# A hybrid decoder layer on one core: copies moved from VectorE to ScalarE, two heads scaled in one product, priorities at stage borders, new step orders

## The chip, the cores and the metric

The kernel runs on one core of one Trainium2 chip. The core has a matrix engine (TensorE, "PE" in the profile, with its weight loads as "PEld"), a vector engine (VectorE, "DVE"), an activation engine (ScalarE, "ACT"), a general engine (GpSimd, "POOL") and an engine that here only issues DMAs (SyncE, "SP"). Each works through its own queue in order; semaphores make one wait for another. PSUM is the memory that matmuls write, in banks; SBUF holds everything else on the chip. The metric is the device time of one launch in microseconds.

## The reference

One layer of a decoder for a prompt of 2048 positions and for 8 sample sequences of 8 new positions, with shared weights, all in float32:

```python
h = rmsnorm(x, g_pre_mix)
proj = h @ w_in                                  # 1024 -> q 512 | k 128 | v 128 | u 512
q, k = rope(q, pos), rope(k, pos)
attn = sink_attention(...)                       # 8 query heads, 2 kv heads of 64, window 128, sinks
pooled = pool_mix(u_ext, pos, pool_w, pool_scale)   # trailing means over 2/4/8/16 minus the token
mix = concatenate([rmsnorm(attn, g_attn), rmsnorm(pooled, g_pool)]) @ w_out
x = x + rmsnorm(mix, g_post_mix)
hf = rmsnorm(x, g_pre_mlp)
ff = square(relu(hf @ w_up)) @ w_down            # 1024 -> 4096 -> 1024
x = x + rmsnorm(ff, g_post_mlp)
x = x + sigmoid(x @ w_ple_gate + b_ple_gate) * (pe @ w_ple)
```

In the softmax every row's sum also holds exp(sink - max). The outputs are both x, and the last 128 keys and values and the last 15 pooling inputs of the prompt and of each sample; the old part of the sample's state is copied over unchanged.

## The kernel before

Float32 products are split: an operand is written as a high part in the engine's short float32 form and a low remainder, and a product is three matmuls, high x high, high x low, low x high (`mm3`, L134 to L136). The splits are a cast on ScalarE (L207) and a subtraction on VectorE (L130).

The work runs in stages, one behind the other.

1. *Mixer* (to about 420 us). 16 prompt tiles of 128 positions, t = 0 to 15, behind the sample tile t = -1. For a tile, `front` does the input projection, keys and values first, then queries, then u, in some 14 steps; `attention` does the scores, the softmax and the products with the values in 6 steps, for the two groups g of four heads; `pooling` has 3 steps, `finish` (called `l` when it belongs to the tile before) 2. In the loop's turn t the front of tile t + 1 is woven with attention and pooling of tile t and the finish of tile t - 1. Which step comes next is written out by hand in strings: ORDER for most tiles, ORDERW for tiles 3 to 10, where the output weights are split and stored as well (`e`), ORDER1 for tile 14, ORDER2 for tile 15, where `e` is the first part of the output product.

   In `front` the transposed keys of a tile go into the right half of `kp`, and the keys of the tile before are copied into its left half (L462, VectorE). In `attention` the exponents `pr` of four heads are scaled by the reciprocal sums `es`, two by VectorE, two by ScalarE (L535, L537). The product with the values, `po`, holds for each group the sums of the high and of the low parts in two halves of 64 partitions; one half is copied to `part` (L560, VectorE), and VectorE adds the other half to it (L561). Banks of PSUM rotate: two for transposes (`tr`), two for scores, two shared by `po`, pooling and the sums of squares (`o`), two for projections.

2. *Output product and first residual* (to about 607 us). `Mixed.product` makes two partial sums per half of the columns; ScalarE scales the first (L252), VectorE the second and adds it (L254). `first_residual` normalizes, adds x and writes the result. The residuals of the last two tiles are late: `residual_late(0)` and `residual_late(1)` are called inside the first round of the next stage, behind its steps p6 and p5.

3. *Up projection* (to about 1262 us). A scheme with seven products in place of eight for a 2 x 2 block matrix. 48 rounds, for three blocks of 352 columns and 16 column pairs of the weights. `up_weights` loads four blocks of a round's weights into `raw`, forms four differences (`diff`, L1016, in block 0) and splits the seven operands. A round runs its products p1, p2, p6, p7, p5 and, behind the next round's p1, the last two (`end`). `ahead`, called at a round's start, prepares the next round's weights. `snap` (L1059) is ScalarE's copy of a partial sum that the same bank goes on adding to, so the next product on that bank waits for it.

4. *Down projection* (to about 1902 us), in the same seven products (`DownQuad`), for 8 groups g of the weights' rows and 8 pairs tp of tiles, a quad each. VectorE adds each result to `z` (L1278). The next group's weights come in from tp = 2 on: two loads (L1211) at tp = 2, two at tp = 4, differences on GpSimd (L1217), splits. The sample rows are done at tp = 2 (`sample_down`, their sums at L1323 and L1325). In group 1 at tp = 3 three DMAs copy the sample's old state to the outputs.

5. *Second residual, gate and embedding* to the end.

Every instruction's place in its engine's queue is decided when the program is built, by a planner that simulates the run: of the instructions that are ready in its simulated time it takes the one that is earliest in the program. Under `tc.high_priority()` an instruction goes before the others that are ready; `tc.keep_in_program_order` pins an instruction behind what its engine was given before. DMAs are issued by SP in its queue's order.

Of the kernel before, what the change touches and what calls it, by code (L numbers as in the profile page):

```python
# [10 lines left out]
F32 = mybir.dt.float32  # L11
# [3 lines left out]
ALU = mybir.AluOpType  # L15
PSUM = bass.MemoryType.PSUM

P = 128
# [24 lines left out]

ORDER = "f f f f l f a f f p a f f f f f a f p f a f f l a a p"

ORDERW = "e a e f f l f f f f p a f f f e f a f f p a f f f f p a a l"
ORDER1 = "f a f f f l a f f f p f a f f f f f p l f a a a p"
ORDER2 = "e a p l a a e l a p e a e p e e"
# [40 lines left out]
def trunk(ctx: ExitStack, tc: tile.TileContext, i: dict, o: dict):  # L89
# [121 lines left out]
    class Mixed:  # L211
# [26 lines left out]
        def product(self, t, nh, bank, into=None):  # L238

            n = tn(t)  # L240
            m, z = self.m[t], self.z[t]
            ns = slice(nh * 512, nh * 512 + 512)
            pab = [bank.tile([P, 512], F32, tag="acc", name="pab") for _ in range(2)]
            for cg in range(2):
                for c in range(4):
                    wk = self.w[cg * 2 + c // 2, nh]
                    a = (m[:, 0, cg * 4 + c], m[:, 1, cg * 4 + c]) if t >= 0 else m[:, 0, cg * 4 + c]
                    mmt(t, pab[cg], a, (wk[:, c % 2, 0], wk[:, c % 2, 1]), c == 0, c == 3)
                if t < 0:
                    fold(into, pab[cg], "s", 2, 2048)  # L250
                if cg == 0:
                    A.mul(out=z[:n, ns], in_=pab[0][:n], mul=rap[:n, t + 1, 0:1])  # L252
                else:
                    V.scalar_tensor_tensor(  # L254
                        out=z[:n, ns], in0=pab[1][:n], scalar=rap[:n, t + 1, 1:2], in1=z[:n, ns], op0=ALU.mult, op1=ALU.add
                    )
                yield
# [16 lines left out]
    with ExitStack() as sa:  # L274
# [111 lines left out]
        def front(t, hT, cs, rs, res):  # L386
            n = tn(t)
# [62 lines left out]
            for j, _ in enumerate(gemm(768, 512, ups)):  # L450
# [3 lines left out]
                if j == 0:  # L454
                    kp = over.pool.tile([P, 4, 256], F32R, tag="kp", bufs=2, name="kp")
                    ps = tr.tile([P, 4, P], F32R, tag="tr", name="trk")
                    for g in range(2):
                        for e in range(2):
                            T.transpose(ps[:, g * 2 + e, :], khl[:, g, 2 * e : 2 * e + 2, :].rearrange("p a d -> p (a d)"), identr)
                    A.copy(out=kp[:, :, P:], in_=ps.bitcast(F32))  # L460
                    if t > 0:
                        V.tensor_copy(kp[:, :, :P], state["kp"][:, :, P:].bitcast(F32))  # L462
                    state["kp"] = kp
                    yield
# [26 lines left out]
        def attention(t, kp, qT, mix, sq):  # L491
# [5 lines left out]
            for g in range(2):  # L497
# [34 lines left out]
                V.reciprocal(es, es)  # L532
                for hh in range(4):
                    if hh % 2:
                        A.mul(out=pr[:, hh, :nkey], in_=pr[:, hh, :nkey], mul=es[:, hh : hh + 1])  # L535
                    else:
                        V.tensor_scalar_mul(pr[:, hh, :nkey], pr[:, hh, :nkey], es[:, hh : hh + 1])  # L537
                prs.append(pr)
                yield
            part = over.pool.tile([P, 4, P], F32, tag="part", bufs=1, name="part")  # L540
            for g in range(2):
# [17 lines left out]
                own, other = slice(g * HD, g * HD + HD), slice(HD - g * HD, 2 * HD - g * HD)  # L559
                V.tensor_copy(part[own], po[other])  # L560
                V.tensor_tensor(out=mix[own, 0:4, :], in0=po[own], in1=part[own], op=ALU.add)  # L561
# [255 lines left out]
    with ExitStack() as sb:  # L817
# [145 lines left out]
        with ExitStack() as s3:  # L963
# [37 lines left out]
            def up_weights(b, j):  # L1001
# [19 lines left out]
                rows(b22, 1, 1)  # L1021
                rows(b21, 1, 0)
                if b == 0:
                    diff(t1, t3, b11)
# [81 lines left out]
            def up_rounds():  # L1106
# [3 lines left out]
                o7s = {}  # L1110

                def prepare(k):
                    if k < len(rounds):
                        held[k] = list(zip(*zip(*(up_weights(b, j) for b, j in rounds[k]))))

# [3 lines left out]
                sp3.n = 1  # L1119
                o7s[0].update(load_ops(0, OPS[5:]))  # L1120

                behind = {
                    0: {"p6": lambda: residual_late(0), "p5": lambda: residual_late(1)},
                    1: {"p6": turn_late, "p5": turn_late},
# [3 lines left out]
                for k, r in enumerate(rounds):  # L1128
                    quads = [UpQuad(b, j, o7s[b], w) for (b, j), w in zip(r, held.pop(k))]
# [72 lines left out]
        with ExitStack() as s4:  # L1202
# [145 lines left out]
            def down_quads():  # L1348
# [4 lines left out]
                def quad(k):  # L1353
# [159 lines left out]
```

## Time and profile before

| | us |
|---|---|
| median of three runs (2151.54 to 2157.3) | 2156.13 |
| the profiled execution | 2156.64 |
| its span in the profile | 2154.9 |

The profile is of one execution. Its first part gives each engine's busy time. A row of the windows view gives, for a stretch from A to B, its length, then busy time (and count of instructions) for PE, PEld, DVE, ACT and POOL, then the granted clock of TensorE as a share of full speed, the DMA engines' busy share and GB/s. A row of the groups view gives line, engine, operation, output <- inputs, shapes and count, then busy time and the mean of one in ns, then the engine's idle time just before them and what ended it. A row of the waits view gives who waited for whom, us in total, how often, and the longest. A row of the timeline gives start, duration and instruction, and in brackets the engine's idle time before it and what ended it. Matmuls overlap: one's duration is longer than the distance from its start to the next one's. A few matmul records are missing from the trace.

### The profile page before, as it was taken

How to read it: one execution, taken by the hardware profiler on the slowest of the kernel's cores; microseconds unless marked ns; L12 is line 12 of the kernel's file. 1: busy time of each engine (PE TensorE's matmuls, PEld its weight loads, DVE VectorE, ACT ScalarE, POOL GpSimd, SP SyncE). 2: the span in 40 equal slices, each digit the busy share in tenths (PEclk: the TensorE clock that was granted, in tenths of full speed). 3: DMA queues.
4: the chain of work that ended last, by engine and by line, in shares of the span. 5: the costliest groups of instructions: out<-in, count | busy, mean ns of one | idle time of the engine just before them, and what ended most of it. 6: DMA issues, size and time to landing. Idle time of an engine off the chain costs nothing. (4 is left out here: it accounts for less than half of the span.)

```text
span 2154.9 us, 31214 instructions
## 1 busy us (share of the span) xinstructions
PE 2129.8 (99%) x11439; PEld 1882.8 (87%) x11439; DVE 1573.8 (73%) x2719; ACT 956.8 (44%) x1864; POOL 576.3 (27%) x643
## 2 busy tenths in 40 slices
PE   8999999999999999999999999999999999999999
PEld 6888888788889999999999988788888888888887
DVE  6899888876688777555755566788888888876553
ACT  5676666545455445444544455233232233232221
POOL 2334343343440000000000035534534544300000
PEclk9999999999999999999999999999999999999999
DMA  7552122768789668666766532231231222342211
GB/s 221 176 174 92 63 70 67 264 220 249 230 259 322 223 217 273 208 191 190 225 197 189 164 111 92 97 101 49 92 99 53 97 91 72 107 138 83 89 54 40
DMA packets 310007, 320.43 MB, mean 149 GB/s; under 512 B 79775, under 2 KB 257247, under 8 KB 302654
## 3 DMA queue, kind: packets, MB, share of 16 engines
q1 hardware_dynamic: 309854, 318.44, 46.7%
q8 instruction: 90, 1.47, 0.3%
q14 instruction: 63, 0.52, 0.1%
HBM read 217.17 MB, written 102.51 MB: 148 GB/s over the span
## 5 line engine op out<-in xcount | busy, mean ns | idle before, releaser
L1278 DVE TENSOR_TENSOR z<-dn,z 128x512 f32<-128x512 f32 x416 | 277.8, 684 | 78.0 <-PE dn L1270 70.1
L130 DVE TENSOR_TENSOR g<-raw,g 128x512 fp32r<-128x512 f32 x336 | 226.8, 694 | 88.9 <-ACT g L207 88.2
L1052 PE MATMUL up<-e,g 128*128 128x352 f32 x832 | 269.5, 324 | 6.0 <-ACT snap L1059 5.8
L1053 PE MATMUL up<-e,g 128*128 128x352 f32 x832 | 267.9, 322 | 0.0
L1054 PE MATMUL up<-e,g 128*128 128x352 f32 x832 | 264.3, 323 | 0.0
L1217 POOL TENSOR_TENSOR raws<-raws 128x1024 f32<-128x1024 f32 x32 | 84.0, 2635 | 617.6 <-DVE wr L130 408.4
L207 ACT CAST g<-raw 128x512 fp32r<-128x512 f32 x336 | 203.8, 623 | 97.4 <-PE up L1054 77.4
L1268 PE MATMUL dn<-wr,ms 128*128 128x512 f32 x512 | 199.3, 390 | 1.5 <-DVE z L1278 1.5
L1269 PE MATMUL dn<-wr,ms 128*128 128x512 f32 x512 | 199.2, 389 | 0.0
L1270 PE MATMUL dn<-wr,ms 128*128 128x512 f32 x512 | 198.2, 389 | 0.0
L1052 PEld LDWEIGHTS up<-e,g 128*128 128x128 f32 x832 | 156.6, 188 | 7.2 <-ACT snap L1059 6.6
L1053 PEld LDWEIGHTS up<-e,g 128*128 128x128 f32 x832 | 157.4, 189 | 0.1
L1054 PEld LDWEIGHTS up<-e,g 128*128 128x128 f32 x832 | 156.0, 189 | 0.0
L1066 DVE TENSOR_TENSOR t<-up,snap 128x352 f32<-128x352 f32 x144 | 71.2, 520 | 115.4 <-ACT snap L1059 100.0
L207 ACT CAST m<-fr 128x512 fp32r<-128x512 f32 (+1 forms) x128 | 65.4, 514 | 194.2 <-PE dn L1270 172.5
L1268 PE MATMUL dn<-wr,m 128*128 128x512 f32 x384 | 149.5, 389 | 1.7 <-DVE z L1278 1.7
L1269 PE MATMUL dn<-wr,m 128*128 128x512 f32 x384 | 149.4, 389 | 0.0
L1270 PE MATMUL dn<-wr,m 128*128 128x512 f32 x384 | 149.3, 389 | 0.0
L848 POOL TENSOR_TENSOR s<-fr 128x256 f32<-128x256 f32 x64 | 54.1, 845 | 308.3 <-DVE ms L130 241.7
L1059 ACT COPY snap<-up 128x352 f32<-128x352 f32 x144 | 61.0, 454 | 165.6 <-PE up L1054 165.6
L207 ACT CAST wr<-raws 128x1024 fp32r<-128x1024 f32 x66 | 69.1, 1050 | 116.5 <-PE dn L1270 57.8
L1268 PEld LDWEIGHTS dn<-wr,ms 128*128 128x128 f32 x512 | 96.1, 188 | 22.1 <-issue 1.9
(279 smaller groups left out, 5725.8 us busy)
## 6 DMA issues: line engine op xcount, KB each, us to landing
raw<-in_w_up_dram SPq DMA_DIRECT2D x160, 256.0 KB, 4.4
raw<-upt SPq DMA_DIRECT2D x32, 1024.0 KB, 7.8
fr<-ffd SPq DMA_DIRECT2D x64, 512.0 KB, 3.5
ffd<-r SPq DMA_DIRECT2D x96, 256.0 KB, 2.9
upt<-raw SPq DMA_DIRECT2D x16, 1024.0 KB, 8.5
raws<-in_w_down_dram SPq DMA_DIRECT2D x32, 512.0 KB, 5.4
sp<-hfd SPq DMA_DIRECT2D x21, 704.0 KB, 6.6
xt<-in_x_t_dram SPq DMA_DIRECT2D x16, 512.0 KB, 5.7
```

The costliest lines, as they stand in the source:

```text
L130: eng.tensor_tensor(out=out, in0=full, in1=hi.bitcast(F32), op=ALU.subtract)
L207: copy(out=dst[:, 0], in_=src)
L1052: T.matmul(ps, l[0], r[0], start=st, stop=False, skip_group_check=not fresh)
L1053: T.matmul(ps, l[0], r[1], start=False, stop=False, skip_group_check=not fresh)
L1054: T.matmul(ps, l[1], r[0], start=False, stop=c == 3, skip_group_check=not fresh)
L1059: A.copy(out=s, in_=ps)
L1066: V.tensor_tensor(out=t, in0=ps, in1=s, op=ALU.add)
L1217: G.tensor_tensor(out=t, in0=x, in1=y, op=ALU.subtract)
L1268: T.matmul(ps, l[0], r[0], start=fresh and j == 0, stop=False, skip_group_check=not fresh)
L1269: T.matmul(ps, l[0], r[1], start=False, stop=False, skip_group_check=not fresh)
L1270: T.matmul(ps, l[1], r[0], start=False, stop=j == 1, skip_group_check=not fresh)
L1278: V.tensor_tensor(out=z, in0=ps, in1=z, op=ALU.add)
```

## The change

Six things are done.

- The three strings of step orders ORDER, ORDERW and ORDER1 are rewritten. The steps are the same.
- The copy of the keys of the tile before (L462) and the copy of po's other half (L560) are made by ScalarE. Of the four scalings by `es`, heads 0 and 1 become one product of 128 x 512 elements with a broadcast operand on VectorE, heads 2 and 3 are ScalarE's.
- The scaling of the output product (L252, L254) and the sample's sums in the down projection (L1323, L1325) get high priority.
- `up_weights` stops once behind its loads, so that they can be called for ahead of the rest. In round 0 `ahead` only begins the loads of round 1; the differences and splits of round 1 are called for behind `residual_late(0)`, after p6 of round 0. In later rounds loads and splits follow each other as before.
- A round's quad is built directly from its one entry; this is the same quad.
- The three state copies move from tp = 3 to tp = 7 of group 1.

```diff
-ORDER = "f f f f l f a f f p a f f f f f a f p f a f f l a a p"
+ORDER = "f f f f l f a f f p p f f f f f f a f p f a f f l a a a"
-ORDERW = "e a e f f l f f f f p a f f f e f a f f p a f f f f p a a l"
-ORDER1 = "f a f f f l a f f f p f a f f f f f p l f a a a p"
+ORDERW = "e a e f f l f f f f p a f f f e f a f f p a f f f f a a p l"
+ORDER1 = "f f a f a l a f f f p f a f f f f f p l f a a f p"
...
-                if cg == 0:
-                    A.mul(out=z[:n, ns], in_=pab[0][:n], mul=rap[:n, t + 1, 0:1])
-                else:
-                    V.scalar_tensor_tensor(
...
+                with tc.high_priority():
+                    if cg == 0:
+                        A.mul(out=z[:n, ns], in_=pab[0][:n], mul=rap[:n, t + 1, 0:1])
+                    else:
+                        V.scalar_tensor_tensor(
...
-                        V.tensor_copy(kp[:, :, :P], state["kp"][:, :, P:].bitcast(F32))
+                        A.copy(out=kp[:, :, :P], in_=state["kp"][:, :, P:].bitcast(F32))
...
-                for hh in range(4):
-                    if hh % 2:
-                        A.mul(out=pr[:, hh, :nkey], in_=pr[:, hh, :nkey], mul=es[:, hh : hh + 1])
-                    else:
-                        V.tensor_scalar_mul(pr[:, hh, :nkey], pr[:, hh, :nkey], es[:, hh : hh + 1])
+                some = pr[:, 0:2, :nkey]
+                V.tensor_tensor(out=some, in0=some, in1=es[:, 0:2].unsqueeze(2).to_broadcast([P, 2, nkey]), op=ALU.mult)
+                for hh in range(2, 4):
+                    A.mul(out=pr[:, hh, :nkey], in_=pr[:, hh, :nkey], mul=es[:, hh : hh + 1])
...
-                V.tensor_copy(part[own], po[other])
+                A.copy(out=part[own], in_=po[other])
...
                 rows(b21, 1, 0)
+                yield
                 if b == 0:
                     diff(t1, t3, b11)
...
+                coming = {}
+
+                def begin(k):
+                    if k < len(rounds):
+                        coming[k] = up_weights(*todo[k])
+                        next(coming[k])
+
                 def prepare(k):
                     if k < len(rounds):
-                        held[k] = list(zip(*zip(*(up_weights(b, j) for b, j in rounds[k]))))
+                        if k not in coming:
+                            begin(k)
+                        held[k] = list(coming.pop(k))
...
+                def late_first():
+                    residual_late(0)
+                    prepare(1)
...
-                    0: {"p6": lambda: residual_late(0), "p5": lambda: residual_late(1)},
+                    0: {"p6": late_first, "p5": lambda: residual_late(1)},
...
-                        prepare(k + 1)
+                        begin(1) if k == 0 else prepare(k + 1)
...
-                    if first and g == 0:
-                        A.copy(out=z, in_=ps)
-                    else:
-                        V.tensor_tensor(out=z, in0=ps, in1=z, op=ALU.add)
+                    with tc.high_priority():
+                        if first and g == 0:
+                            A.copy(out=z, in_=ps)
+                        else:
+                            V.tensor_tensor(out=z, in0=ps, in1=z, op=ALU.add)
...
-                        if g == 1 and tp == 3:
+                        if g == 1 and tp == 7:
                             queue(o["new_k_sample"][0, :, : WIN - TDEC], i["state_k"][0, :, TDEC:])
```

More of the change, by code (lines that the diff above doesn't have):

```diff
@@ L42 @@
 C_COLS = C_HOT + 4
-ORDER = "f f f f l f a f f p a f f f f f a f p f a f f l a a p"
-ORDERW = "e a e f f l f f f f p a f f f e f a f f p a f f f f p a a l"
-ORDER1 = "f a f f f l a f f f p f a f f f f f p l f a a a p"
+ORDER = "f f f f l f a f f p p f f f f f f a f p a f f l a a a"
+ORDERW = "e a e f f l f f f f p a f f f e f a f f p a f f f f a a p l"
+ORDER1 = "f f a f a l a f f f p f a f f f f f p l f a a f p"
 ORDER2 = "e a p l a a e l a p e a e p e e"
@@ L250, in product @@
                     fold(into, pab[cg], "s", 2, 2048)
-                if cg == 0:
-                    A.mul(out=z[:n, ns], in_=pab[0][:n], mul=rap[:n, t + 1, 0:1])
-                else:
-                    V.scalar_tensor_tensor(
-                        out=z[:n, ns], in0=pab[1][:n], scalar=rap[:n, t + 1, 1:2], in1=z[:n, ns], op0=ALU.mult, op1=ALU.add
-                    )
+                with tc.high_priority():
[3 more added lines that the diff above has]
+                        V.scalar_tensor_tensor(
+                            out=z[:n, ns], in0=pab[1][:n], scalar=rap[:n, t + 1, 1:2], in1=z[:n, ns], op0=ALU.mult, op1=ALU.add
+                        )
                 yield
@@ L1128, in up_rounds @@
                 for k, r in enumerate(rounds):
-                    quads = [UpQuad(b, j, o7s[b], w) for (b, j), w in zip(r, held.pop(k))]
+                    quads = [UpQuad(*r[0], o7s[r[0][0]], held.pop(k))]
                     def ahead(k=k, b=r[-1][0], j=r[-1][1]):
-                        prepare(k + 1)
+                        begin(1) if k == 0 else prepare(k + 1)
                         if j == DFF // 256 - 2 and b + 1 < N_BLOCKS:
```

## The prediction

> **What bounds the kernel now.** I read the page's busy times first, then PE's busy time in stretches of 25 us, then PE's waits, then the timeline around each stretch that is not full.
>
> ```profile
> PE 2129.8 (99%) x11439; PEld 1882.8 (87%) x11439; DVE 1573.8 (73%) x2719; ACT 956.8 (44%) x1864; POOL 576.3 (27%) x643
> ...
> 0.00:25.00 25.00, 19.35 (x83) 12.10 (x84) 15.17 (x25) 16.75 (x24) 4.90 (x16) 1.00 0.92 284
> ...
> 300.00:325.00 25.00, 25.00 (x164) 22.45 (x163) 22.26 (x67) 17.80 (x48) 10.90 (x15) 1.00 0.33 104
> ...
> 375.00:400.00 25.00, 21.62 (x130) 18.98 (x129) 20.89 (x63) 16.15 (x46) 8.34 (x11) 0.86 0.75 290
> 400.00:425.00 25.00, 24.40 (x136) 20.60 (x135) 22.00 (x45) 13.74 (x29) 9.32 (x9) 1.00 0.69 247
> ...
> 550.00:575.00 25.00, 24.49 (x116) 20.11 (x115) 15.16 (x14) 13.06 (x22) 9.70 (x12) 1.00 0.80 258
> ...
> 600.00:625.00 25.00, 20.63 (x108) 18.72 (x107) 19.95 (x23) 11.57 (x20) 13.48 (x12) 0.93 0.97 303
> ...
> 1250.00:1275.00 25.00, 23.45 (x125) 20.62 (x124) 20.31 (x27) 14.66 (x24) 10.97 (x13) 1.00 0.50 146
> ...
> 1375.00:1400.00 25.00, 21.76 (x95) 17.24 (x94) 22.28 (x29) 5.40 (x9) 12.25 (x12) 1.00 0.14 43
> ...
> 2150.00:2154.90 4.90, 0.27 (x3) 0.07 (x1) 1.27 (x3) 0.42 (x1) 0.00 (x0) 0.87 0.15 54
> ```
>
> TensorE is the bound: its matmuls fill 2129.8 of 2154.9 us. The change takes none of them away, so all it can win is what TensorE loses around them. A stretch of 25 us that shows 25.00 has nothing to give. The five stretches of the middle that do not are the whole field: idle 3.38 + 0.60 us where the mixer ends (375 to 425), 0.51 us in the output product, 4.37 us where the up projection begins, 1.55 us where the down projection begins, 3.24 us in that projection's second group. The start (5.65 us) and the tail (4.63 us) are touched by no edit.
>
> Two of these places cost a second time, in the clock column.
>
> ```profile
> 612.44 0.32 PE L1053 MATMUL up<-e,g 128*128 128x352 f32 x1
> 612.60 0.32 PE L1054 MATMUL up<-e,g 128*128 128x352 f32 x1
> ...
> 618.75 0.49 PE L1052 MATMUL up<-e,g 128*128 128x352 f32 x1
> 619.04 0.49 PE L1053 MATMUL up<-e,g 128*128 128x352 f32 x1
> ```
>
> Before the gap the same product starts every 0.16 us, after it every 0.29 us. A granted clock of 0.86 and 0.93 over 25 us loses at most 0.14 x 25 = 3.5 us and 0.07 x 25 = 1.75 us. So the ceilings are 3.98 + 3.5 = 7.5 us for the mixer's end, 4.37 + 1.75 = 6.1 us for the start of up, and 0.51, 1.55 and 3.24 us for the rest: 18.9 us, 0.9% of the run.
>
> **The change part by part.** *The mixer's arithmetic (L462, L537, L560).*
>
> ```profile
> L560 DVE COPY part<-po 64x512 f32<-64x512 f32 x32 | 22.0, 689 | 9.9 <-PE po L558 9.3
> L462 DVE CAST kp<-kp 128x512 fp32r<-128x512 f32 x15 | 8.1, 541 | 9.9 <-ACT kp L460 9.8
> L537 DVE TENSOR_SCALAR pr<-pr,es 128x256 f32<-128x256 f32 x60 | 24.1, 443 | 0.6
> L130 DVE TENSOR_TENSOR qhl<-qr,qhl 128x512 fp32r<-128x512 f32 x16 | 10.9, 682 | 0.1
> L621 ACT COPY mix<-pq 128x512 f32<-128x512 f32 x16 | 9.4, 587 | 8.0 <-PE pq L136 7.8
> L207 ACT CAST m<-fr 128x512 fp32r<-128x512 f32 x64 | 39.7, 621 | 156.4 <-PE dn L1270 134.6 <-DMA fr<-ffd 16.0 <-DVE z L1278 5.8
> ...
> L462 DVE CAST kp<-kp x15: 410/423/1473, 57.4 to 369.1; 128x512 fp32r<-128x512 f32 x15
> ```
>
> The key copy comes once per tile, so 14 steps between 57.4 and 369.1 us make a tile 22.3 us. Per tile VectorE loses 0.54 us (key copy) and 2 x 0.689 = 1.38 us (po). The four scalings were 24.1 / 15 = 1.61 us; two products of 128x512 from SBUF, by the nearest row 0.682 us each, are 1.36: 0.25 us less. Together 2.2 us of the 19.9 that it is busy per tile (22.26 of 25 us). ScalarE gains 0.62 us and 2 x 0.587 = 1.17 us: 1.8 us on 15.9 (17.80 of 25 us), 79% in place of 71%. ScalarE's copy from 64 partitions of PSUM is in no row; bounds are 0.50 us (L520's activation of half the free size, quoted with the rivals) and the 0.69 us that VectorE needs; I take 0.587, whose source and free size are the same. TensorE is full in this stage, so all this is worth 0 us there; its cover is that TensorE has a front of the next tile to run.
>
> Here a rule speaks against the change. The Trainium skill, "VectorE: DVE Perf Modes", section "Why `tensor_tensor` can't do 2×_2P or 4×", says that a float32 scaling by a per-partition scalar moves two elements per cycle and a product of two tensors one. An estimate by its 0.96 GHz is 512 / 0.96 = 533 ns for the new product and 267 ns for the two scalings that it replaces, both before fixed costs, so by that page the fusion is a loss of up to 0.27 us a product. The rows (402 to 443 ns a scaling, 682 ns a product) put the fixed cost and waits higher than the rule's gain; by the rule the sum of VectorE's relief would be about 1.4 us a tile in place of 2.2, and the time the same, since this stage is not VectorE's.
>
> *The step orders and the mixer's end.* ORDER1 puts the last but one tile's attention forward: its third step comes behind the third step of the front in place of the eighth, its fourth behind the seventh in place of the last. ORDER and ORDERW move pooling or attention by a few steps. No instruction is added.
>
> ```profile
> PE trk L459 <- DVE pt L130: 1.3, 1, 1.3
> ...
> PE trp L547 <- ACT ux L581: 0.7, 1, 0.7
> ...
> PE trq L470 <- DVE pt L130: 0.7, 1, 0.7
> ...
> PE trp L547 <- ACT pr L535: 0.7, 1, 0.7
> ...
> 389.85 0.66 PE L547 MATMUL trp<-ident,pr 128*128 128x128 f32 x4 [0.71 <-ACT ux L581]
> 391.85 0.53 PE L459 MATMUL trk<-identr,khl 128*128 128x128 f32 x4 [1.34 <-DVE pt L130]
> ...
> 402.24 0.39 PE L134 MATMUL pab<-wo,ms 128*128 128x512 f32 x1
> ```
>
> From where the last front runs out to the first output product (402.24) TensorE has only attention and pooling of the last two tiles, and each short wait is for VectorE or ScalarE to give back a transpose bank. Attention that is done sooner and VectorE relieved of 2.2 us a tile shorten this tail. But the last tile's own chain (transpose, scores, exponent, scale, transpose, product) is left, with nothing else to run until the output weights land, and ScalarE, now carrying three more copies per tile, is in it three times. Bounds: -2 us (three waits of 0.7 us more) and +7.5 us (all of it). I take 3.0: half of the idle time, 2.0 us, and some 1 us of the 3.5 at the low clock. In the full part of the mixer, where TensorE has nothing to win back, the new order is bounded by 0 and by -3 us (four of the 14 tiles with one wait of 0.7 us as above); I take 0.
>
> *Scaling of the output product at high priority (L252, L254).* It gives the PSUM bank back sooner; PE waited once, 0.51 us, for ScalarE's scaling. I take 0.5, bounds 0 and 0.5. What it passes, the residual's work, has VectorE at 15.16 of 25 us as cover.
>
> *Weights of the second up round begun early, finished behind the late residual.*
>
> ```profile
> 614.90 1.06 ACT L183 ACTIVATE z<-xt 128x1024 f32<-128x1024 f32 x1 [5.32 <-DVE xt L875]
> ...
> 615.96 1.35 ACT L207 CAST l<-sp 128x1408 fp32r<-128x1408 f32 x1
> 617.21 0.44 ACT L1059 COPY snap<-up 128x352 f32<-128x352 f32 x1
> ...
> 612.38 1.29 DVE L1016 TENSOR_TENSOR raw<-raw 128x512 f32<-128x512 f32 x2 [1.22 <-DMA raw<-in_w_up_dram]
> 613.59 1.22 DVE L875 TENSOR_TENSOR xt<-xt,z 128x1024 f32<-128x1024 f32 x1
> ...
> 608.84 2.32 DVE L874 SCALAR_TENSOR_TENSOR z<-z,rsq,g_post_mix 128x1024 f32<-128x1024 f32 x1
> ...
> 617.71 0.66 PE L1052 MATMUL up<-e,g 128*128 128x352 f32 x1 [4.30 <-ACT snap L1059]
> ```
>
> Read upward: PE waits for a snap that stands behind a square (L183) in ScalarE's queue, the square for L875 in VectorE's, and L875 behind differences (L1016) that wait for the weights' DMA. The change keeps the four loads at their place in SP's queue and puts the differences and the seven splits behind the residual. Then L875 can follow L874 at 611.2, ends by 612.4 in place of 614.8, and with 1.06 + 1.35 + 0.44 us behind it the snap ends at 615.1; without the difference ahead of L874 (0.86 us) nearer 614. So 2.5 to 3.5 us of the 4.3 go, and with a gap of about one us the low clock, 1.75 us, probably too. What is late next is the second round's first split: VectorE is full from 612 on (19.95 of 25 us with its own 3 us of waiting). Bounds 0 and 6.1; I take 4.5.
>
> *Down projection: state copies moved from the fourth quad of group 1 to its last, sample sums at high priority.*
>
> ```profile
> 1362.51 0.95 SPq L1211 DMA_DIRECT2D raws<-in_w_down_dram  x2
> ...
> 1374.48 2.33 DVE L130 TENSOR_TENSOR wr<-raws,wr 128x1024 fp32r<-128x1024 f32 x1 [3.40 <-ACT wr L207]
> ...
> 1377.56 0.47 PE L1268 MATMUL dn<-wr,ms 128*128 128x512 f32 x1 [1.54 <-DVE z L1278]
> ...
> 1459.64 2.23 DVE L130 TENSOR_TENSOR wr<-raws,wr 128x1024 fp32r<-128x1024 f32 x1
> ```
>
> Three copies (2.0 us of issuing on SP) go from before the weight loads of quad 4 to a point with no weight load left in the group; next in SP's queue are only operand loads. In group 1 a weight split stands in VectorE's queue ahead of the sums and waits 3.40 us; in group 2, where there are no copies, its like waits for nothing. I take 3.0 (that group 1 becomes like group 2), bounds -2 (operand loads late behind the copies) and 3.24. The gap of 1.55 us at 1262 is no edit's: 0, bounds -1 and 1.5.
>
> **Sum**: 3.0 + 0.5 + 4.5 + 3.0 = 11 us. The profiled execution took 2156.64 us, 1.7 over its span and 0.5 over the median 2156.13: 2156.6 - 11 = 2145.6, say **2146 us**.
>
> **The rivals.** *The half clock goes whole.* At the mixer's end the gaps are 0.7 to 1.3 us each. The Trainium skill, "TensorE: Matmul & The Clock Gate", Part 1, has the clock fall after an idle window of about 3.4 us and rise after a busy one. The rows that bear it out: 0.86 and 0.93 beside the two widest losses, 1.00 beside the 3.24 us at 1377. If the waits thin out enough, all 7.5 us come back there in place of 3.0: 2141, with the rest as forecast. Against: the chain of the last tile stays.
>
> *The waits only move.* VectorE is full after 612, the last tile's chain stays, and the wait in group 1 was the order of VectorE's queue and not the copies: 1 + 0.5 + 2.5 + 0 = 4 us, 2152.6. For it: the copies had been issued 4 us before the weights, whose way from SP to VectorE, 1362.5 to 1374.5 us, is as long as group 2's.
>
> *ScalarE becomes the mixer's bound, slower.* A po bank is now freed by a copy that stands behind ScalarE's exponents, four of 0.50 us with reads of 0.19, some 2.4 us. PE has two such banks for four uses a tile, one in 22.3 / 4 = 5.6 us, so it decides only when a copy is more than about 5 us late; for it speaks 79% busy in order, against it the idle 21% and that no wait for po's bank shows now. Price: 0.8 us at each of 30 copies, 24 us, less the 8 us of the other places: 2173.
>
> ```profile
> L520 ACT ACTIVATE pr<-pr,nm 128x256 f32<-128x256 f32 x120 | 60.1, 504 | 25.0 <-DVE nm L509 25.0
> ```
>
> **How the numbers follow.** A measurement tells about 0.3% (6.5 us) from no change. Chances: forecast 0.48, clock 0.12, waits that move 0.31, ScalarE 0.09. Faster are the first two, 0.60; same 0.31; slower 0.09. The range takes the clock rival with 3 us more of the bounds (2138) and the rival of the moved waits with the -3 us of the mixer's neighbours and -4 us of bounds elsewhere (2160); outside are ScalarE's case and the tips, under 0.2.
>
> **What would show it.** Right: windows 375 to 425 with under 2.5 us idle, no PE wait for a snap above 1.5 us near 613, clock 1.00 there, full windows from 1375 to 1400, VectorE some 2 us a tile lower and ScalarE 1.8 higher, windows of 25.00 between 75 and 375. Wrong: PE waiting for ScalarE's part or for po in the mixer, a new wait of PE on a split near 620, or the wait for z at the start of group 2.

## The result and the profile after

| | us |
|---|---|
| before, median of 6 runs (2151.54 to 2157.3) | 2153.57 |
| after, median of 6 runs (2164.74 to 2174.64) | 2168.21 |
| ratio after / before, 95% interval | 1.0065 (1.0054 to 1.0076) |
| span of the profiled execution, before / after | 2154.9 / 2167.3 |

The change makes the kernel 0.65% slower. The forecast was 11 us faster, and its range ended at 2160. First the page's busy times and the stretches of 25 us of the kernel after (columns as in the part on the profile before):

```profile
PE 2131.7 (98%) x11439; PEld 1881.2 (87%) x11439; DVE 1562.5 (72%) x2640; ACT 983.4 (45%) x1911; POOL 580.0 (27%) x643
```

```profile
350.00:375.00 25.00, 23.51 (x145) 20.12 (x144) 18.52 (x49) 16.61 (x44) 9.29 (x12) 1.00 0.23 71
375.00:400.00 25.00, 20.76 (x117) 17.05 (x116) 19.54 (x51) 18.14 (x45) 9.96 (x12) 0.83 0.85 335
...
450.00:475.00 25.00, 23.81 (x117) 18.73 (x116) 19.95 (x20) 11.70 (x21) 14.61 (x16) 1.00 0.61 202
475.00:500.00 25.00, 23.39 (x110) 18.58 (x109) 17.02 (x16) 10.72 (x19) 12.18 (x14) 1.00 0.73 218
500.00:525.00 25.00, 23.33 (x111) 19.11 (x109) 14.11 (x14) 10.62 (x18) 5.31 (x12) 1.00 0.68 195
525.00:550.00 25.00, 23.87 (x112) 19.52 (x112) 15.32 (x14) 14.17 (x23) 9.56 (x13) 1.00 0.88 262
550.00:575.00 25.00, 22.59 (x99) 18.36 (x100) 16.77 (x15) 13.02 (x21) 10.88 (x13) 0.93 0.87 281
...
625.00:650.00 25.00, 19.95 (x117) 19.36 (x116) 22.88 (x31) 14.47 (x27) 6.07 (x7) 0.93 0.84 289
...
1375.00:1400.00 25.00, 23.14 (x101) 18.28 (x99) 20.86 (x24) 5.24 (x7) 15.82 (x11) 1.00 0.25 85
```

TensorE's busy time has grown by 1.9 us (2131.7 for 2129.8) and the span by 12.4, so 10.5 us are idle time. Before, the output product (425 to 600 us) had one stretch that was not full; now five in a row from 450 us on lose 1.1 to 2.4 us each. The mixer's end is no better (4.24 us idle in 375 to 400 for 3.38), the start of up neither (5.05 for 4.37), and only group 1 of the down projection has gained (1.86 for 3.24). PE's waits in the kernel after say on what:

```profile
PE pab L134 <- ACT z L253: 6.8, 5, 2.4
PE up L1053 <- ACT snap L1060: 4.7, 2, 3.2
PE po L557 <- ACT pt L549: 3.9, 3, 1.5
PE dn L1282 <- DVE z L1292: 2.0, 3, 1.7
...
PE up L1055 <- DVE g L130: 1.9, 1, 1.9
...
PE pab L134 <- DVE z L255: 1.2, 1, 1.2
```

The first line is the scaling of the output product, the very step that was given priority: 6.8 us, where before it was 0.5. PE has run out of accumulators, since the scaling that frees them stands in ScalarE's queue behind work of the residual. The timeline of the kernel after, ScalarE's and PE's rows at the longest of these waits:

```profile
519.12 1.03 ACT L207 CAST ms<-mr 128x1024 fp32r<-128x1024 f32 x1
523.24 1.36 ACT L207 CAST e<-sp 128x1408 fp32r<-128x1408 f32 x1 [3.09 <-DMA sp<-hfd]
524.51 0.58 ACT L891 COPY h<-trx 128x512 f32<-128x512 f32 x1
524.99 1.27 ACT L253 ACTIVATE z<-pab,rap 128x512 f32<-128x512 f32 x2
...
525.73 0.50 PE L134 MATMUL pab<-wo,ms 128*128 128x512 f32 x1 [2.40 <-ACT z L253]
```

ScalarE idles 3.09 us for an operand that the residual has written out and that is read back, and the scaling stands behind it. The kernel before has the same order here (its cast idled 2.74 us), but its residual was further ahead. Where the residual fell behind is seen in SP's queue and on VectorE. First the timeline of before, SP's rows and one of VectorE, then that of after, SP's rows and two of VectorE:

```profile
425.69 0.32 SPq L637 DMA_DIRECT2D mixd<-mix  x1
429.60 0.60 SPq L230 DMA_DIRECT2D mr<-mixd  x1
430.28 0.61 SPq L178 DMA_DIRECT2D g_post_mix<-in_g_post_mix_dram  x1
...
434.76 0.33 SPq L230 DMA_DIRECT2D mr<-mixd  x1
...
436.08 1.29 DVE L874 SCALAR_TENSOR_TENSOR ez<-ez,rsq,g_post_mix 128x1024 f32<-128x1024 f32 x1 [1.35 <-POOL rsq L143]
```

```profile
430.35 0.59 SPq L230 DMA_DIRECT2D mr<-mixd  x1
431.08 0.57 SPq L637 DMA_DIRECT2D mixd<-mix  x1
436.07 0.32 SPq L230 DMA_DIRECT2D mr<-mixd  x1
436.48 0.38 SPq L178 DMA_DIRECT2D g_post_mix<-in_g_post_mix_dram  x1
...
434.82 1.23 DVE L130 TENSOR_TENSOR ms<-mr,ms 128x1024 fp32r<-128x1024 f32 x1 [0.25 <-ACT ms L207]
...
442.28 1.28 DVE L874 SCALAR_TENSOR_TENSOR ez<-ez,rsq,g_post_mix 128x1024 f32<-128x1024 f32 x1 [6.17 <-DMA g_post_mix<-in_g_post_mix_dram]
```

A second load of a mixer result (mr, that of tile 4) now stands ahead of the gains. Its slot comes free when VectorE has split the result that lay in it (434.82 + 1.23 us, the issue is at 436.07), so the gains are issued at 436.48 in place of 430.28, and the first product with the gain starts at 442.28 (before 436.08). The 97th accumulator product, taken as a mark of how far TensorE has come in this stage, starts only 2.3 us later than before (434.9 for 432.6): the residual lies 7.3 us behind it and no longer 3.5.

### The profile page after: what moved, and what is told of

Its sections match the earlier page's. It is cut to its first block, busy times and chain, and to the rows that moved or that the text cites. A ratio compares the mean times of both kernels' runs of the same rounds, so it can differ in the third digit from the quotient of the medians.

```text
span 2167.3 us, 31162 instructions
## 1 busy us (share of the span) xinstructions
PE 2131.7 (98%) x11439; PEld 1881.2 (87%) x11439; DVE 1562.5 (72%) x2640; ACT 983.4 (45%) x1911; POOL 580.0 (27%) x643
## 5 line engine op out<-in xcount | busy, mean ns | idle before, releaser
L141 POOL TENSOR_SCALAR rst<-ss 128x1 f32<-128x1 f32 (+1 forms) x68 | 21.4, 315 | 350.4 <-ACT ms L183 211.4
```

## The experiments

The idle time of PE in four stretches tells the stages apart: length less PE's busy time in the windows view, from 75 to 375 us (mixer), 375 to 450 (its end), 450 to 600 (output product), 600 to 700 (start of up). "Gain" is the start of the first product with the gain less that of the 97th accumulator product. Each ratio is to the kernel before on the same chip.

| kernel | median us | ratio (95%) | 75-375 | 375-450 | 450-600 | 600-700 | gain |
|---|---|---|---|---|---|---|---|
| before | | | 0.2 | 4.0 | 0.5 | 4.5 | 3.5 |
| after | 2168.2 | 1.0065 (1.0054-1.0076) | 2.2 | 5.0 | 8.0 | 5.4 | 7.3 |
| a_no_order | 2162.7 | 1.0032 (1.0017-1.0046) | 0.9 | 5.9 | 1.2 | 4.9 | 3.3 |
| a_no_order1 | 2162.7 | 1.0027 (1.0017-1.0037) | 2.0 | 6.1 | 0.9 | 4.2 | 3.5 |
| a_no_act | 2173.6 | 1.0082 (1.0066-1.0098) | 6.0 | 11.4 | 0.6 | 4.6 | 2.5 |
| a_no_z | 2168.1 | 1.0051 (1.0035-1.0068) | 2.2 | 5.0 | 7.5 | 4.2 | 7.3 |
| a_no_up | 2171.9 | 1.0067 (1.0049-1.0085) | 2.3 | 4.8 | 6.8 | 5.2 | 7.4 |
| a_gain_first | 2169.5 | 1.0056 (1.0041-1.0071) | 2.7 | 5.1 | 6.7 | 4.6 | 7.5 |
| a_mr3 | 2164.2 | 1.0039 (1.0025-1.0054) | 2.0 | 3.7 | 4.2 | 5.4 | 3.5 |
| a_gain_ahead | 2165.4 | 1.0039 (1.0024-1.0055) | 1.9 | 5.0 | 2.4 | 4.3 | 3.3 |
| b_act | 2164.6 | 1.0038 (1.0027-1.0049) | 0.9 | 6.8 | 2.1 | 4.3 | 3.3 |
| b_kp_part | 2164.7 | 1.0036 (1.0024-1.0047) | 2.1 | 5.4 | 3.4 | 4.2 | 7.5 |
| b_heads | 2169.9 | 1.0050 (1.0027-1.0073) | 2.8 | 6.0 | 4.3 | 4.6 | 7.6 |
| b_order1 | 2159.3 | 1.0012 (1.0003-1.0022) | 0.5 | 5.6 | 0.5 | 4.8 | 3.5 |
| b_up_down | 2154.6 | 0.9993 (0.9983-1.0002) | 0.0 | 3.8 | 1.5 | 4.2 | 3.5 |
| b_pin2 | 2160.0 | 1.0020 (1.0008-1.0033) | 0.1 | 4.9 | 0.6 | 5.2 | 3.5 |
| b_down | 2152.7 | 0.9987 (0.9977-0.9997) | 0.0 | 3.8 | 0.4 | 4.1 | 3.5 |
| b_cp (one run) | 2154.2 | | 0.0 | 4.0 | 0.6 | 4.6 | 3.5 |

Names that begin with a_ are the kernel after with one part undone or added, those with b_ the kernel before with one part of the change or an addition.

**Which part of the change costs.** Five undo one part each, two of them the strings:

```diff
 a_no_order1 (a_no_order: ORDER and ORDERW too)
-ORDER1 = "f f a f a l a f f f p f a f f f f f p l f a a f p"
+ORDER1 = "f a f f f l a f f f p f a f f f f f p l f a a a p"
 a_no_act
-                A.copy(out=part[own], in_=po[other])
+                V.tensor_copy(part[own], po[other])
 (the copy of kp and the four scalings as before, too)
 a_no_z
-                with tc.high_priority():
                     if cg == 0:
 a_no_up
-                        begin(1) if k == 0 else prepare(k + 1)
+                        prepare(k + 1)
...
                     residual_late(0)
-                    prepare(1)
```

> The changed kernel with the step strings ORDER, ORDERW and ORDER1 of before; all else as changed. Theory L (the last tile's attention ends 5.4 us later, so SP's queue issues the loads of the residual's two gains 6.2 us later, and the output-product stage runs behind its accumulators): if the strings made the last tile late, the store of the last mixer result comes back from 431.1 to about 426 us, the gain loads from 436.5 to about 430, PE's waits of 2.4 and 2.35 us at 525 and 564 go, and the time falls by about 10 to 12 us, to 2156 to 2159. Theory Z (the priority on the scaling of the output product costs the 12 us by itself): time stays within 4 us of 2168. Theory A (the work moved to ScalarE makes the last tile late): store at 431 still, time within 4 us of 2168.

> The changed kernel with the string of tile 14 (ORDER1) of before, ORDER and ORDERW as changed. With it the planner puts the gains' loads ahead of the load that waits for its slot, as in the kernel before. If the new ORDER1 is what made the last tile late and so cost the 5 to 6 us that undoing all three strings gave: 2161 to 2164, last accumulator of the output product near 612 us. If ORDER and ORDERW cost it (the front arrives at tile 14 with less of the attention done): within 3 us of 2168.

> The changed kernel with the copies of the other half of po and of the last tile's keys on VectorE and the heads scaled one by one as before; orders and priorities as changed. Theory A: the last mixer result is stored at about 426 us instead of 431, the output-product stage loses its 12 us, 2156 to 2159. Theory L by the strings: the store stays at 431 or comes later, and the 6 us that tiles 1 to 13 of the mixer are ahead of before stay or go; time within 4 us of 2168.

> The changed kernel without the priority on the scaling of the output product. Theory Z: the 12 us between the first and the last accumulator of the output product come back, 2156 to 2158. Theories L and A: the order of ScalarE's and VectorE's queues in this stage is nearly the same with and without the priority, so the time stays within 3 us of 2168, the gain loads stay at 436 us.

> The changed kernel without the split preparation of the up weights (the next round is prepared whole, the late residual of the first round without the preparation of round 1). All theories: the waits of 3.2 and 1.9 us near 620 us become the one of 4.30 us of before, so the time changes by -1 to +2 us from 2168. If the split instead pushes work into the end of the output-product stage and so costs part of the 12 us there, the last accumulator comes earlier than 619.5 us and the time falls by more than 3 us.

The strings cost 0.33%, 7 us, and as far as the intervals tell ORDER1 is all of it (undoing it alone gives 0.38%): with the old ORDER1 alone the gains' loads stand ahead of the load for tile 4 again, the residual lies 3.5 us behind, and the output product is idle 0.9 us. (The store of the last mixer result came no earlier than after, against the expectation; only the order of the two loads changed.) Without the priority only a few instructions change places, none of them ahead of 618 us, so the queues of the output product are those of the kernel after, and it idles 7.5 us as against 8.0: theory Z falls, and the priority moves nothing in this stage. Without the split preparation of the up weights the order of all five queues is that of the kernel after, instruction for instruction: this part of the change moves nothing, and the two rows of the table (8.0 and 6.8 us idle, 1.0065 and 1.0067) show how far two measurements of one order lie apart. Undoing the work on ScalarE makes the kernel slower still. PE's waits from 375 to 450 us in a_no_act:

```profile
PE pss L633 <- POOL sq L629: 6.2, 1, 6.2
PE po L559 <- DVE pt L130: 2.5, 2, 1.3
PE pab L134 <- DVE ez L255: 1.7, 1, 1.7
```

With the new strings and the old arithmetic the last tile's sum of squares becomes the wait, 6.2 us. So undoing a part doesn't give back what the part costs: each sets the planner on another order.

**Whether the late gains are the cause.** Three try to bring them forward:

```diff
 a_gain_first
-            gpost, gmlp = rows_of(p2, "g_post_mix"), rows_of(p2, "g_pre_mlp")
+            gpost, gmlp = rows_of(p2, "g_post_mix", G), rows_of(p2, "g_pre_mlp", G)
-                SY.dma_start(xt[:n], xrows(t))
+                (G if t in (0, 1) else SY).dma_start(xt[:n], xrows(t))
 a_mr3
-            raw = self.mrp.tile([P, 8, P], F32, tag="mr", bufs=2, name="mr")
+            raw = self.mrp.tile([P, 8, P], F32, tag="mr", bufs=3, name="mr")
 a_gain_ahead (gate[0] is the DMA of the second gain)
-            SY.dma_start(raw[:, :, :n], mixd[t])
+            with tc.issue_after(gate[0]) if t == 4 else nullcontext():
+                SY.dma_start(raw[:, :, :n], mixd[t])
```

> The changed kernel with the two gains and x of the first two residuals loaded by GpSimd's queue in place of SP's, where they stood behind the load of a later tile's mixer result (436.1 us) that waits for its slot. Theory L (a residual that starts late makes the scaling late and TensorE run out of accumulators): the gains are issued near 432 us instead of 436.5, the first product with the gain starts at 437 to 438 instead of 442.3, PE's waits for the scaling on ScalarE (6.8 us in all, longest 2.4) fall under 2 us, and the time falls by 5 to 8 us, to 2160 to 2163. Theory T (the loss in this stage has another cause, such as the order in which ScalarE's queue takes scaling, squares and casts): the residual starts earlier, the waits at 473 to 565 us stay within 2 us of 6.8 in all, time within 3 us of 2168.

> The changed kernel with three slots in place of two for the loaded mixer results, so that the load ahead of the gains in SP's queue has no slot to wait for. Theory L (the residual that starts late costs the output-product stage its 6 to 8 us of waits): gains issued 3 to 5 us sooner against the first accumulator, PE's waits for the scaling (6.8 us on ScalarE, 1.2 on VectorE) fall under 3 us, time 2161 to 2164. Rival (the waits have their cause in the order of ScalarE's queue and not in the late start): waits above 6 us stay, time 2166 to 2170.

> The changed kernel with one edge in SP's queue: the load of the mixer result of tile 4 goes behind the loads of the two gains, as it does in the kernel before. Nothing else of the program changes. Theory L: the first product with the gain comes 3.5 us behind the 97th accumulator product instead of 7.3, the stretch from the 201st to the last accumulator product takes 149 to 151 us instead of 159, and the time falls by 6 to 9 us, to 2159 to 2162. Rival (the late start is only a sign of a slower queue order on ScalarE and VectorE): the stretch stays at 155 to 159, time 2165 to 2169.

The first is a miss that tells nothing: on GpSimd the loads stood behind the last tile's own work and were issued at 441.98 us, as late against the accumulators (7.5 us) as after. a_gain_ahead adds one edge to SP's queue; the planner then swaps a few neighbours on the other engines, too (about four pairs on ScalarE and eight on VectorE). From its waits between 440 and 620 us, and one stretch:

```profile
PE pab L134 <- ACT z L256: 2.4, 4, 0.8
```

```profile
450.00:600.00 150.00, 147.56 (x703) 120.50 (x702) 101.60 (x91) 74.44 (x121) 65.25 (x80) 1.00 0.77 230
```

The waits for the scaling go from 8.0 us (6.8 and 1.2) to 2.4, and the idle time of the stage from 8.0 to 2.4. The three kernels that have this stage in the order of after (after, a_no_z, a_no_up) idle 8.0, 7.5 and 6.8 us, so 4.4 to 5.6 us go with that load's place in the queue. By the ratios (1.0065, 1.0051 and 1.0067 to 1.0039) the time falls by 2.6 to 6 us, at or below the 6 to 9 expected; the intervals overlap. a_mr3, which takes away what that load waits for, comes to the same ratio with 4.2 us idle, though its gains are as early as before (3.5). So the late gains do not explain the rest: x of the first residual landed late as well (VectorE waited 2.20 us for it in a_gain_ahead), but what that costs was not tried.

**The work on ScalarE by itself, and the string by itself,** on the kernel before:

```diff
 b_kp_part
-                        V.tensor_copy(kp[:, :, :P], state["kp"][:, :, P:].bitcast(F32))
+                        A.copy(out=kp[:, :, :P], in_=state["kp"][:, :, P:].bitcast(F32))
...
-                V.tensor_copy(part[own], po[other])
+                A.copy(out=part[own], in_=po[other])
 b_heads
+                some = pr[:, 0:2, :nkey]
+                V.tensor_tensor(out=some, in0=some, in1=es[:, 0:2].unsqueeze(2).to_broadcast([P, 2, nkey]), op=ALU.mult)
 (heads 2 and 3 on ScalarE; b_act: both of these; b_order1: the new ORDER1 alone)
```

> The kernel before with the mixer's arithmetic of the change alone: copies of po's other half and of the last tile's keys on ScalarE, heads 0 and 1 in one product. If these help as the undoing in the changed kernel says (it became 5 us slower without them): 2151 to 2154 against 2156 or 2157 of before. If they cost the 4 us that are left at the mixer's end without the new strings (PE waited 3.4 us there for the two-head product and 2.5 for VectorE's pt): 2159 to 2163.

> The kernel before with the two copies alone on ScalarE (po's other half, the keys of the tile before); heads scaled one by one as before. All three pieces together cost 8.6 us. If the copies on ScalarE cost it (they stand behind exponents in its queue, and po's bank is given back later): 2162 to 2165, with PE waiting for ScalarE at the last two tiles. If the two-head product costs it: 2154 to 2158.

> The kernel before with heads 0 and 1 scaled in one product of 128 x 512 on VectorE and heads 2 and 3 on ScalarE; the copies stay on VectorE. If this costs most of the 8.6 us (the first transposes of tile 15 wait for a product of 0.69 us behind VectorE's queue; PE waited 3.5 us for it): 2161 to 2165, with that wait of PE at 389 us. If the copies cost it: 2154 to 2158.

> The kernel before with the new step string of tile 14 (ORDER1) alone. If that string costs the 5.5 us that its undoing gave in the changed kernel, whatever stands beside it: 2160 to 2162, with the late gains (first product with the gain 7 us behind the 97th accumulator product). If it costs only together with the work moved to ScalarE: within 2 us of before.

Each loses: copies 0.36%, product 0.50%, both together 0.38%. Copies alone and product alone each make the gains late (7.5 and 7.6 us) and idle 3.4 and 4.3 us in the output product; together they don't, and lose at the mixer's end. (Nor do late gains have one price: at 7.3 us the kernel after idles 8.0.) At the mixer's end, in b_act (PE's waits from 375 to 420 us):

```profile
PE trp L546 <- DVE pr L534: 3.5, 1, 3.5
PE trk L459 <- DVE pt L130: 3.4, 1, 3.4
```

The three waits of 0.7 to 1.3 us for a transpose bank are now two of 3.5 and 3.4: the two-head product stands behind four maxima of the next group in VectorE's queue. That it is one product for two heads is not the cause: in b_kp_part, which scales head by head, PE waits 4.0 us for the like scaling (`trp <- DVE pr L537`). ORDER1 alone costs 0.12%, 2.6 us, most of it at the mixer's end (5.6 us idle), with the gains on time. So the greater part of its 7 us in the changed kernel comes only in combination with the other parts.

In one order of steps the ratios do add up. The arithmetic alone (b_act) stands at 1.0038; with the state copies, which give back about 0.001 (next part), that is 1.0028, and the change without its ORDER1 (a_no_order1) measured 1.0027. ORDER1 on top makes it 1.0065. By this the moved arithmetic costs about 8 us, ORDER1 on top of it another 8, and the state copies give back 2, each to some 3 us.

**The start of up, and the down projection.**

```diff
 b_pin2 (added[t] is the addition of x in the residual of tile t)
                 if b == 0:
-                    diff(t1, t3, b11)
+                    with tc.issue_after(added[NT - 2].ins) if j == 2 else nullcontext():
+                        diff(t1, t3, b11)
...
 b_cp
-                        if g == 1 and tp == 3:
+                        if g == 1 and tp == 7:
 b_down: b_cp with the priority of the sample sums
 b_up_down: b_down with begin, prepare and late_first of the change
```

> The kernel before with the up and the down part of the change alone (begun loads, late splits, state copies at the eighth quad, sample sums first). As my prediction has it: 4.5 and 3.0 us less, 2149. By the traces of the changed kernel: the wait of 4.30 us at the start of up is replaced by waits of 3.2 and 1.9 us, so nothing there, and one of two waits in group 1 of the down projection goes, 1.5 us: 2155 to 2156, no difference that can be measured.

> The kernel before with one thing changed: the four weight differences of round 2 of the up projection are queued on VectorE behind the addition of x in the first late residual. Reading of the queues: the differences that stand between the product with the gain and that addition belong to round 2 (their loads go out before round 1's, because their slot is free first), and the change moved only round 1's, so VectorE's queue stayed as it was. If that is right, the wait of 4.30 us of PE for the snap falls to 1 to 2 us and the time by 2.5 to 4.5 us, to 2152 to 2153.5. Rival, the waits only move (VectorE is full behind 612 us and the first split of round 1 or 2 comes late): PE waits for a split of g for as long as it gained, time within 1.5 us of before.

> The kernel before with the down projection's edits alone (state copies at the eighth quad, sample sums first). By the traces one of the two waits in group 1 shrinks by 1.1 to 1.4 us and nothing else moves: 1 to 1.5 us less than before, 2154 against 2155.5. If these edits were worth the 3.0 us of the prediction: 2152.5.

> One look at the kernel before with only the state copies moved to the eighth quad of group 1. If the copies on SP delay the weights of group 2: VectorE's split at about 1374 us waits 2.0 us instead of 3.4 and PE's wait of 1.54 us there is under 0.3. If the priority of the sample sums does it: both as before.

The timeline of b_up_down, VectorE's rows, and its wait of PE:

```profile
611.19 2.32 DVE L874 SCALAR_TENSOR_TENSOR z<-z,rsq,g_post_mix 128x1024 f32<-128x1024 f32 x1
614.55 1.29 DVE L1016 TENSOR_TENSOR raw<-raw 128x512 f32<-128x512 f32 x2 [1.05 <-DMA raw<-in_w_up_dram]
615.76 1.22 DVE L875 TENSOR_TENSOR xt<-xt,z 128x1024 f32<-128x1024 f32 x1
```

```profile
PE up L1053 <- ACT snap L1060: 4.1, 1, 4.1
```

Nothing has moved: the differences still stand between the product and the addition, and the wait is 4.1 us for 4.3. In all five queues b_up_down, b_down and b_cp have one order, and it differs from that of before in the three state copies of SP's queue alone. If these differences belong to round 2, as the expectation of b_pin2 reads the queues, then the change postponed those of round 1, which stood behind the residual already. b_pin2 postpones round 2's. Its VectorE and GpSimd rows, then its waits from 600 to 700 us:

```profile
604.72 2.31 DVE L876 SCALAR_TENSOR_TENSOR z<-z,rsq,g_post_mix 128x1024 f32<-128x1024 f32 x1 [2.19 <-POOL rsq L143]
607.07 2.20 DVE L877 TENSOR_TENSOR xt<-xt,z 128x1024 f32<-128x1024 f32 x1
...
605.91 2.28 POOL L848 TENSOR_TENSOR s<-h 128x512 f32<-128x512 f32 x1
608.27 2.16 POOL L849 TENSOR_TENSOR s<-s,h 128x512 f32<-128x512 f32 x1
```

```profile
PE up L1055 <- ACT snap L1062: 2.6, 1, 2.6
PE up L1055 <- ACT g L207: 2.3, 2, 2.0
```

Now the addition follows the product, so the differences between them were round 2's. The wait for the snap falls to 2.6 us, but PE waits 2.3 us for a weight split, and the kernel is 0.2% slower. So the three state copies are all that is left of this part. Their order was measured twice, at 0.9993 (0.9983 to 1.0002) and 0.9987 (0.9977 to 0.9997), and b_cp, timed once, at 2154.23 us: about 0.1% faster than before, at the edge of what these rounds can tell, and the only part of the change that shows any gain. The timeline of b_cp, PE's rows in group 1:

```profile
1375.14 0.47 PE L1268 MATMUL dn<-wr,ms 128*128 128x512 f32 x1 [0.79 <-DVE z L1278]
1378.46 0.47 PE L1268 MATMUL dn<-wr,m 128*128 128x512 f32 x1 [1.69 <-DVE z L1278]
```

The wait of 1.54 us is halved (0.80 in b_down), the one of 1.70 behind it stays. The way can be followed back. GpSimd's first difference of these weights and VectorE's split, in the timeline of before, then in that of b_cp:

```profile
1368.50 10.56 POOL L1217 TENSOR_TENSOR raws<-raws 128x1024 f32<-128x1024 f32 x4 [5.03 <-DMA raws<-in_w_down_dram]
```

```profile
1365.89 10.74 POOL L1217 TENSOR_TENSOR raws<-raws 128x1024 f32<-128x1024 f32 x4 [3.73 <-DMA raws<-in_w_down_dram]
...
1372.07 2.32 DVE L130 TENSOR_TENSOR wr<-raws,wr 128x1024 fp32r<-128x1024 f32 x1 [2.65 <-ACT wr L207]
```

The weights' load is issued at 1362.51 us before and at 1361.20 in b_cp, so GpSimd, which waits for it, starts 6.0 us after the issue with the copies ahead of it and 4.7 us without. That distance is 4.9, 4.7 and 4.6 us in b_down, b_up_down and the kernel after, and 5.2 to 6.8 in the five other kernels that were made from before and keep the copies at the fourth quad. VectorE's split then waits 2.65 us in place of 3.40, which are the 0.75 us that PE gains; the expectation had 2.0.

## Why the prediction was wrong

- *Output product, "I take 0.5, bounds 0 and 0.5".* This is the step that failed with the greatest loss. The bound came from the wait that showed there, as if a stage could only get back what it lost. The working did not ask what else the new orders would re-plan: the stage lost 7.5 us, of which 4.4 to 5.6 go with one load that the planner put ahead of the gains. The same holds for the sentence over all terms, that all the change can win is what TensorE loses around its matmuls: no term had room for a loss in a stage that had been full.
- *The mixer's arithmetic, "worth 0 us there".* The working looked for its price in the full part of the mixer alone and for a gain at the end. By itself (b_act) it costs 0.38%, 8 us: the idle time rises by 0.7 us from 75 to 375, by 2.8 at the mixer's end, by 1.5 in the output product and by 2.5 in the down projection, where none of its instructions stands.
- *The mixer's end, -3.0 (bounds -2 and 7.5).* It came out at +1.0 us idle (5.0 for 4.0). The waits did not thin out, they changed names (pt on ScalarE, 2.5 us, for three transpose banks; of the four waits quoted for banks, the one on `pr` was for an operand). The rival of ScalarE as the bound comes near the time (2173 for 2168) by luck: PE waits 3.9 us in all for ScalarE's pt in the mixer, but neither b_act nor the kernel after has a wait for po's bank, which was its mechanism. In the full part the loss is 1.9 us, inside the bound of 3 that was not taken.
- *Start of up, -4.5.* Nothing, as no queue changed: the differences that I saw ahead of L875 were taken for round 1's without looking which round they belong to. And when they are moved, b_pin2 shows the rival "the waits only move" to be right here.
- *Down projection, -3.0.* Mechanism right, size too large: the state copies delay the weights behind them and are worth 0.75 us of PE's wait in b_cp (1.54 less 0.79), but group 1 doesn't become like group 2: the split still waits 2.65 us, and the second wait of 1.7 was never theirs.
- *Arithmetic.* The copy of po on ScalarE took 0.582 us (forecast 0.587), the two-head product 0.750 (0.682). With no GpSimd work beside them the product took 690 ns and a scaling of one head 347, so the fusion saved nothing. VectorE's relief of 2.2 us a tile came out at 0.7 by its busy time in the whole kernel (from 1573.8 to 1562.5 us, 11.3 over 15 to 16 tiles); from 75 to 375 us, 13 tiles of 22.3 us, it is about 1 (269.56 to 255.33). Small operations grew, as the next but one part shows. ScalarE gained 1.7 us a tile (956.8 to 983.4), for the 1.8 forecast.
- *Priority of the scaling:* no instruction of the output product changes its place by it. *Gap at 1262, 0:* right.

## What to carry to other kernels

Where a planner orders the queues, an edit is not local: compare each engine's queue before and after, the DMA queue first, before the arithmetic is weighed. A load that waits for its slot holds back the loads behind it in the queue (here the gains by 6.2 us), so look at what stands behind such a load, and pin those that start a chain ahead of it. And a stall's cause is named by the buffer in its way, not by the line: the same line serves several rounds.

## What the hardware showed that was not expected

Many of VectorE's instructions with two operands in SBUF are stretched beside GpSimd's. The groups view from 75 to 400 us, before and then after, the sum `es`:

```profile
L531 DVE TENSOR_TENSOR es<-es,sm 128x4 f32<-128x4 f32 x28 | 7.3, 262 | 6.0 <-ACT es L530 6.0
```

```profile
L532 DVE TENSOR_TENSOR es<-es,sm 128x4 f32<-128x4 f32 x29 | 13.4, 463 | 4.9 <-ACT es L531 4.8
```

Sorted by whether a GpSimd instruction lies beside it, the sum of 128 x 4 elements takes 159 ns on average alone (15 times) and 704 ns beside one (17 times) in the kernel after; the addition `mix<-po,part`, which reads PSUM, 683 and 692. In b_pin2 the addition of x took 2.20 us beside GpSimd's two sums, in b_up_down 1.22 with nothing beside it. Not every one is stretched: of the four additions of x that lie beside GpSimd's work in b_pin2, two kept 1.22 us. The Trainium skill, "SBUF — State Buffer", section "Who interferes with whom", says that the two engines share a pair of ports under an exclusive lock; the durations here agree.

One execution's profile also carries a start of its own. b_up_down and b_down have the same order of instructions, and this is their stretch from 25 to 75 us, first b_up_down, then b_down:

```profile
25.00:75.00 50.00, 49.13 (x303) 39.84 (x302) 30.02 (x104) 21.73 (x62) 19.27 (x26) 0.90 0.51 159
```

```profile
25.00:75.00 50.00, 49.15 (x339) 40.54 (x338) 35.04 (x124) 25.46 (x70) 18.60 (x26) 1.00 0.56 176
```

A granted clock of 0.90 in place of 1.00 over 49 us is 4.9 us, more than most parts of this change are worth. The two profiles at the top differ in this way too: the clock is 0.93 from 25 to 75 us before and 1.00 after, and 1.00 and 0.93 from 0 to 25; by the same working, an estimate, the start of the kernel after is some 2 us the shorter for it, and the spans' difference of 12.4 us too small by as much. So spans of two profiles are to be compared stage by stage.
